# Starting five output groups of the second branch's projection among its last attention head

## The chip, the cores and the metric

The kernel runs on one core of a Trainium2 chip. The core has five engines: TensorE (PE, matrix products and their weight loads, PEld), VectorE (DVE), ScalarE (ACT), GpSimd (POOL) and SyncE (SP, which issues the transfers here). The metric is the time of one execution on the device in microseconds (us); lower is better.

## The reference

Two layers of a transformer-like trunk over 512 latent tokens and 256 context tokens of width 1024. Each layer has two parallel attention branches that share one input projection; each branch is gated and projected, and the two are merged and projected once more:

```python
def _merge(a_att, b_att, a_z, b_z, g_a, g_b, w_o_a, w_o_b, w_out):
    o_a = (a_att * jax.nn.silu(a_z)) @ w_o_a
    o_b = (b_att * jax.nn.silu(b_z)) @ w_o_b
    merged = jax.nn.sigmoid(g_a) * o_a + jax.nn.sigmoid(g_b) * o_b
    return merged @ w_out
```

Branch A is neighbourhood attention with 8 heads of width 64. Branch B is grouped-query attention with 8 query heads and 2 key/value heads; its latent queries read all 768 tokens. In the first layer the context tokens go through the same computation and read only context; in the second only the latent tokens are updated. The output is the 512 latent tokens.

## The kernel before

All matrices are kept as a high and a low part (`hi`, `lo`), and a product is three matmuls: hi x hi, hi x lo, lo x hi (`mm3`, lines 341 to 343). A 512-column matmul fills one bank of PSUM, the accumulator memory, which has eight. Activations stand with channels on the 128 partitions, so that the 512 channels of a branch are four row tiles k = 0 to 3, and `hilo` makes the two parts of a row tile: a copy on ACT (line 543, `gbh` for branch B) and a subtraction on POOL (line 544, `gbl`). `load_w2` loads weights and splits them in the same way; the lo part alternates between POOL and DVE (line 328).

**The last stage of a layer.** The 8 query heads of branch B go through `pipeline`. Head h's scores (lines 704 and 705, into score tiles `pss` of two banks each, two buffers) are computed while head h - 1's values are: for each of six key tiles, four transposes on PE into a `pst` bank (line 655), a hi copy on ACT (`pth`, 658), a lo subtraction on DVE (`ptl`, 659), and two value matmuls that add to the one `psv` bank (958 and 959). At the end of a head `head_out` copies half of `psv` on ACT (667), adds on DVE (668), which frees the bank, and multiplies into `zb` on POOL (669). Two heads make one row tile of `zb`, so that its fourth tile is whole only after head 7, the last. In the first layer each head also has context queries, with a score tile, two values matmuls of 256 columns for each half (732 and 733), and a `head_out` of their own. Between heads PE does pieces of a list of other projections, `fill`, each piece in the one `psf` bank. After the fill has run out, `early` makes hi and lo parts of row tiles 0 to 2.

**The second output projection** (`w_o_b`) comes next, in a new set of banks: `open_ps(x=5)` closes the score and values pools and gives five banks `psx` besides `psf`. Its output has eight row tiles f; with the column spans (0 to 512, and 512 to 768 in the first layer) that is 16 output groups in the first layer and 8 in the second. A group is `chan_proj`: k = 0 to 3, three matmuls each, then `evac_b` on DVE and ACT, which takes the bank with `tg` (lines 993 and 994) and makes the hi and lo parts of the merged activations (`mh`, `ml`). Then follows the final projection (`w_out`, `tok_proj`, also `psf` and `psx` banks).

The order in the program is not the order in which Python calls are made: a scheduler puts the instructions of each engine in an order by its own timeline, and each engine then runs its list strictly in that order, waiting where a source is not ready or a buffer not free. With it, the group in the `psf` bank stood among the last heads' values before the change already.

Of the kernel before, what the change touches and what calls it, by code (L numbers as in the profile page):

```python
# [11 lines left out]
ALU = mybir.AluOpType  # L12
# [27 lines left out]
def R(ap):  # L40
    return ap.bitcast(F32R)
# [7 lines left out]
def hybrid_kernel(es: ExitStack, tc, x, ctx, cvec, w_ada, w_ada0, small, gvec, w_in, w_o_a, w_o_b, w_out,  # L49
                  bias_int, bias_edge, rope, ident_d, out):  # L50
    nc = tc.nc
    V, S, G, T = nc.vector, nc.scalar, nc.gpsimd, nc.tensor
# [265 lines left out]
    def load_w2(src, col0, nk, lo_eng):  # L318

        res = []  # L320
        for i in range(nk // 2):
            raw = raw_tile()
            nc.sync.dma_start(raw.rearrange("p (k n) -> p k n", k=2),
                              src[256 * i:256 * i + 256, col0:col0 + 256].rearrange("(k p) n -> p k n", k=2))
            hi = wp.tile([128, 512], F32R, tag="whi", name=nm("whi"), bufs=8)
            S.copy(hi, raw)  # L326
            lo = wp.tile([128, 512], F32R, tag="wlo", name=nm("wlo"), bufs=8)
            lo_eng(i).tensor_tensor(lo, raw, F(hi), ALU.subtract)  # L328
            res += [(hi[:, c:c + 256], lo[:, c:c + 256]) for c in (0, 256)]
        return res  # L330
# [3 lines left out]
    mix_lo = lambda k: V if k % 2 == 1 else G  # L334
# [23 lines left out]
    def chan_proj(w, f, a, n0, n1, evac):  # L358

        ps = psw(n1 - n0)  # L360
        nk = len(w)
        for k in range(nk):
            hi, lo = a(0, k), a(1, k)
            mm3(ps, (w[k][0][:, 128 * f:128 * f + 128], w[k][1][:, 128 * f:128 * f + 128]),
                (R(hi[:, n0:n1]), R(lo[:, n0:n1])), k == 0, k == nk - 1)
        evac(f, n0, n1, ps)

    def start_mods(q):
        cuts = (0, 256, 512, 768) if q == 0 else (0, 768)
# [23 lines left out]
    def run(fill, n):  # L393
        for _ in range(min(n, len(fill))):
            fill.pop(0)()
# [80 lines left out]
    def layer(l, hx, nxt, mid):  # L476
# [4 lines left out]
        spans = [(0, 512), (512, 768)] if first else [(0, 512)]  # L481
# [53 lines left out]
        gated = {}  # L535

        def hilo_tiles(name):
            return [big(name + part).rearrange("p (f n) -> p f n", f=4) for part in "hl"]

        def hilo(src, dst, fs):  # L540
            sv = src.rearrange("p (f n) -> p f n", f=4)
            for f in fs:
                S.copy(R(dst[0][:, f, :ntok]), sv[:, f, :ntok])
                G.tensor_tensor(R(dst[1][:, f, :ntok]), sv[:, f, :ntok], dst[0][:, f, :ntok], ALU.subtract)
# [4 lines left out]
        def o_chunks(br, prepare, evac):  # L549

            src = (w_o_a if br == "a" else w_o_b)[l]
            act = lambda part, k: gated[br][part][:, k, :]
            res = []
            for i in range(4):
                st = {}

                def ld(i=i, st=st):
                    st["w"] = load_w2(src, 256 * i, 4, mix_lo)
                pieces = [lambda f=f, n0=n0, n1=n1, i=i, st=st:
                          chan_proj(st["w"], f, act, n0, n1, lambda f, a, b, ps: evac(2 * i + f, a, b, ps))  # L560
                          for f in range(2) for n0, n1 in spans]
                res.append((ld, ([prepare] if i == 0 and prepare else []) + pieces))
            return res
# [9 lines left out]
        def tg_part(c, f, n0, n1):  # L573
            return tg[2 * (f // 4) + c].rearrange("p (f n) -> p f n", f=4)[:, f % 4, n0:n1]
# [7 lines left out]
        if first:  # L582
            w, pss = [], [psw() for t in range(6)]
# [19 lines left out]
        else:  # L603
            hp["p"] = bgp_es.enter_context(tc.tile_pool(name=f"cp{l}", bufs=1, reuse_waits="tile"))
            w = load_w(W, C_AK, 512, KT, mix_lo)
# [30 lines left out]
        if True:  # L636
# [183 lines left out]
                head_out(po, e, zv[64 * e:64 * e + 64, h // 2, 0:512])  # L820
                return vsl

            def pipeline(fill, spread, scores_of, values_of, last=None, bg=[]):

                n = len(fill)
                prev = None
                for h in range(8):
                    att["bg"] = bg if h > 3 or pm["n"] == 1 else []
                    st = scores_of(h)
                    if prev is not None:  # L830
                        values_of(h - 1, prev)
                    run(fill, len(fill) - (n - n * min(h + 1, spread) // spread))
                    prev = st
                if last is not None:
                    run(fill, len(fill))
                    last()
                run(bg, len(bg))
                values_of(7, prev)
                run(fill, len(fill))

            akt = [k_tile(e, True) for e in range(2)]

# [8 lines left out]
            def values_of(dst, f):  # L851
                def g(h, st):
                    vsl = f(h, st[0])
                    if first:
                        e = h % 2
                        zv = dst.rearrange("p (f n) -> p f n", f=4)
                        ctx_values(st[1], vsl, zv[64 * e:64 * e + 64, h // 2, 512:768], e)
                return g
# [116 lines left out]
                gated["b"] = hilo_tiles("gb")  # L975
                hilo(zb, gated["b"], range(3))
            bg = gate_steps((1,), att["p"]) if first else []
            pipeline(fill, 8, gq_first, values_of(zb, gq_values), early, bg)
            gq_es.close()

        with tc.tile_pool(name=f"mrg{l}", bufs=1, reuse_waits="tile") as mp:
            open_ps(x=5)
            extra = lambda name: mp.tile([128, 3072], F32, tag="extra", name=nm(name))
            gv = mp.tile([128, nv, DM], F32, tag="gate", name=nm("gate"), bufs=1)
            for v in range(nv):
                src = gd[l][8 * v:8 * v + 8].rearrange("k p -> (k p)").unsqueeze(0)
                nc.sync.dma_start(gv[:, v, :], src.to_broadcast([128, DM]))
            hilo(zb, gated["b"], [3])
            mg = []

            def evac_b(f, n0, n1, ps):
                a, b = tg_part(0, f, n0, n1), tg_part(1, f, n0, n1)
                V.scalar_tensor_tensor(b, b, 1.0, ps, ALU.add, ALU.mult)
                V.tensor_tensor(a, a, b, ALU.add)
                hi, lo = [m[:, f % 4, n0:n1] for m in mg[f // 4]]
                S.copy(R(hi), a)
                V.tensor_tensor(R(lo), a, hi, ALU.subtract)
            chunks = o_chunks("b", None, evac_b)
            chunks[0][0]()
            for i in range(4):  # L1000
                if i < 3:
                    chunks[i + 1][0]()
                if i % 2 == 0:
                    mg.append(hilo_tiles("m"))
                for piece in chunks[i][1]:
                    piece()

            nt = 6 if first else 4
            xv = [a.rearrange("p (t n) -> p t n", t=3) for a in (big("xt0"), extra("xt1"))]
            xts = []  # L1010
            for t in range(nt):
                xt = xv[t // 3][:, t % 3, :]
                nc.sync.dma_start(xt, x_src(t) if first else xs1[128 * t:128 * t + 128, :])
                xts.append(xt)
            a_m = lambda part, k: mg[k // 4][part][:, k % 4, :]
            bg = ada_steps(1, range(16), (1,), 2, mp) + [lambda: ada_mod(1)] if first else []
            run(bg, 1)
            per_bg = -(-len(bg) // nt)
# [123 lines left out]
```

## Time and profile before

| | |
|---|---|
| timed runs | 1154.26, 1154.82 and 1156.4 us; median 1154.82 |
| profiled execution, first to last instruction (span) | 1153.4 us; its own time is not listed apart, the median of the runs is 1.4 us longer than the span |
| mean granted TensorE clock | 0.998 of full speed |
| PE busy | 1123.0 us, 97% of the span |
| DVE, ACT, POOL busy | 809.8, 573.9, 495.0 us |

The last head of branch B ends at about 567 us of the span in the first layer and at about 1085 us in the second. In the lines of the profile, a timeline row gives start and duration in us, engine, line, operation, output <- inputs, shape, and in brackets how long the engine idled before it and what ended that. Matmuls are pipelined: their rows overlap, and the step from one start to the next is what a matmul costs PE. PE counts as busy while one of its matmuls is in flight. A row of windows gives the stretch, its length, then busy time and count of PE, PEld, DVE, ACT and POOL, the granted clock, the share of the DMA engines and GB/s.

### The profile page before, as it was taken

The numbers are of one execution on the slowest core, as the hardware profiler recorded it, in microseconds if no ns is written. First come the engines' busy times: TensorE is split into PE (matmuls) and PEld (weight loads), VectorE is DVE, ScalarE is ACT, GpSimd is POOL, SyncE is SP. The second block draws the span as 40 slices with busy tenths as digits, with TensorE's granted clock in tenths as the row PEclk, the third lists the DMA queues.
The fourth block names the chain that finished last, engine by engine and source line by source line (L and its number), as shares of the span: only waits on it lengthen the run. The fifth ranks groups of instructions, "written<-read, shape, count | busy, mean of one in ns | idle before, by whom it ended". The sixth has DMA issues, their size and how long they took to land.

```text
span 1153.4 us, 17280 instructions
## 1 busy us (share of the span) xinstructions
PE 1123.0 (97%) x6078; PEld 949.0 (82%) x6078; DVE 809.8 (70%) x1508; ACT 573.9 (50%) x1167; POOL 495.0 (43%) x459
## 2 busy tenths in 40 slices
PE   5999999999999999999999999999999999999998
PEld 4688888889988888878788787888888988887786
DVE  4566688897464687688587755469787665898563
ACT  5453266666433465566330265346666445766521
POOL 3362354454375243354411126245553664465311
PEclk9999999999999999999999999999999999999999
DMA  9644222233342332470353523543332333142143
GB/s 368 195 126 137 69 85 65 72 115 97 115 130 63 107 102 73 67 276 19 121 172 101 174 74 110 176 106 113 108 105 84 110 101 101 65 173 92 63 129 92
DMA packets 88000, 134.04 MB, mean 116 GB/s; under 512 B 10629, under 2 KB 52585, under 8 KB 86249
## 3 DMA queue, kind: packets, MB, share of 16 engines
q1 hardware_dynamic: 87912, 132.94, 36.8%
q8 instruction: 48, 0.79, 0.3%
q14 instruction: 40, 0.32, 0.1%
HBM read 115.58 MB, written 17.32 MB: 115 GB/s over the span
## 4 chain that ended last, share of the span: by engine, by line
PE 83%; DVE 7%; issue 3%; POOL 2%; ACT 2%; DMA 2%; ACTq 0%; POOLq 0%; DVEq 0%
PE psx L341 12%; PE psx L343 12%; PE psx L342 12%; PE psf L341 9%; PE psf L342 9%; PE psf L343 9%; PE pst L655 5%; PE pss L704 2%; PE pss L705 2%; PE psv L959 2%; PE psv L958 1%; PE pss L781 1%; PE pst L417 1%; DVE wlo L328 1%; DVE ptl L659 1%
## 5 line engine op out<-in xcount | busy, mean ns | idle before, releaser
L659 DVE TENSOR_TENSOR ptl<-pst,pth 128x512 fp32r<-128x512 f32 (+1 forms) x176 | 116.0, 672 | 46.4 <-ACT pth L658 45.4
L658 ACT CAST pth<-pst 128x512 fp32r<-128x512 f32 (+1 forms) x176 | 99.2, 576 | 87.5 <-PE pst L655 56.3
L328 POOL TENSOR_TENSOR wlo<-raw,whi 128x512 fp32r<-128x512 f32 x68 | 95.0, 1402 | 108.9 <-ACT whi L326 87.8
L341 PE MATMUL psf<-hx,whi 128*128 128x512 f32 (+1 forms) x368 | 139.2, 378 | 0.0
L342 PE MATMUL psf<-hx,whi 128*128 128x512 f32 (+1 forms) x368 | 138.1, 375 | 0.0
L343 PE MATMUL psf<-hx,wlo 128*128 128x512 f32 (+1 forms) x368 | 137.8, 374 | 0.0
L341 PE MATMUL psx<-whi,hx 128*128 128x512 f32 (+1 forms) x368 | 137.2, 374 | 0.0
L342 PE MATMUL psx<-wlo,hx 128*128 128x512 f32 (+1 forms) x368 | 135.8, 369 | 0.0
L343 PE MATMUL psx<-whi,hx 128*128 128x512 f32 (+1 forms) x368 | 133.6, 369 | 0.0
L314 POOL TENSOR_TENSOR wlo<-raw,whi 128x512 fp32r<-128x512 f32 x44 | 60.4, 1373 | 140.4 <-ACT whi L311 123.8
L311 ACT CAST whi<-raw 128x512 fp32r<-128x512 f32 x96 | 58.7, 623 | 103.5 <-PE psx L343 38.6
L326 ACT CAST whi<-raw 128x512 fp32r<-128x512 f32 x136 | 82.5, 622 | 50.3 <-DMA raw<-in_w_in_dram 34.1
L655 PE MATMUL pst<-ident,p 128*128 128x128 f32 x640 | 99.9, 272 | 1.4 <-DVE ptl L659 0.9
L328 DVE TENSOR_TENSOR wlo<-raw,whi 128x512 fp32r<-128x512 f32 x68 | 70.2, 1033 | 28.3 <-ACT whi L326 27.8
L655 PEld LDWEIGHTS pst<-ident,p 128*128 128x128 f32 x640 | 77.7, 141 | 13.3 <-DVE ptl L659 1.6
L644 POOL TENSOR_SCALAR r<-r 128x1 f32<-128x1 f32 x64 | 23.1, 361 | 151.7 <-DVE r L639 144.1
L645 POOL TENSOR_TENSOR p<-p,r 128x512 f32<-128x512 f32 (+1 forms) x64 | 83.5, 1304 | 5.0
L341 PEld LDWEIGHTS psx<-whi,hx 128*128 128x128 f32 x368 | 69.6, 189 | 11.8 <-issue 0.8
L343 PEld LDWEIGHTS psf<-hx,wlo 128*128 128x128 f32 x368 | 69.4, 188 | 11.8
L343 PEld LDWEIGHTS psx<-whi,hx 128*128 128x128 f32 x368 | 69.4, 189 | 11.5
L342 PEld LDWEIGHTS psx<-wlo,hx 128*128 128x128 f32 x368 | 69.6, 189 | 11.0
L341 PEld LDWEIGHTS psf<-hx,whi 128*128 128x128 f32 x368 | 69.4, 189 | 10.8 <-ACT zt L502 0.2
(239 smaller groups left out, 3033.4 us busy)
## 6 DMA issues: line engine op xcount, KB each, us to landing
raw<-in_w_in_dram SPq DMA_DIRECT2D x168, 256.0 KB, 2.9
rawb<-in_w_ada_dram SPq DMA_DIRECT2D x64, 256.0 KB, 2.8
gs<-zt SPq DMA_DIRECT2D x32, 256.0 KB, 2.0
raw<-in_w_out_dram SPq DMA_DIRECT2D x32, 256.0 KB, 2.8
tg<-gs SPq DMA_DIRECT2D x4, 1536.0 KB, 7.4
rawx<-in_w_ada_dram SPq DMA_DIRECT2D x4, 1024.0 KB, 7.2
rawy<-in_w_ada_dram SPq DMA_DIRECT2D x4, 1024.0 KB, 12.2
raw<-in_w_o_a_dram SPq DMA_DIRECT2D x16, 256.0 KB, 2.7
```

The lines of the kernel that those rows point to most:

```text
L311: S.copy(hi[:, :n], raw[:, :n])
L314: e.tensor_tensor(lo[:, :n], raw[:, :n], F(hi[:, :n]), ALU.subtract)
L326: S.copy(hi, raw)
L328: lo_eng(i).tensor_tensor(lo, raw, F(hi), ALU.subtract)
L341: T.matmul(ps, lhs[0], rhs[0], start=first, stop=False)
L342: T.matmul(ps, lhs[0], rhs[1], start=False, stop=False)
L343: T.matmul(ps, lhs[1], rhs[0], start=False, stop=last)
L644: G.tensor_scalar(r[:, i:i + 1], r[:, i:i + 1], 0.5, None, ALU.mult)
L645: G.tensor_tensor(p[:, c0:c1], p[:, c0:c1], r[:, i:i + 1].to_broadcast([128, c1 - c0]), ALU.mult)
L655: T.transpose(pt[:, c0:c0 + 128], src, ident)
L658: S.copy(hi[:, n0:n1], pt[:, n0:n1])
L659: V.tensor_tensor(lo[:, n0:n1], pt[:, n0:n1], F(hi[:, n0:n1]), ALU.subtract)
```

## The change

`chan_proj` is split, so that a group can be begun with some row tiles and ended later (`chan_mm`). `pipeline` gets a `tail`, called after the last head's values. There, still with the pools of the attention stage, `begin_b` opens five groups: one in the `psf` bank, and one each in halves of score tiles. It issues row tiles 0 to 2 of each. Then come the hi and lo parts of row tile 3, and for each of the five its last row tile and its evacuation. The other groups follow as before in the new set of banks, with weights loaded one chunk ahead.

```diff
+    def chan_mm(ps, w, f, a, n0, n1, k0, k1):
+        for k in range(k0, k1):
             hi, lo = a(0, k), a(1, k)
             mm3(ps, ...)
...
                 values_of(7, prev)
                 run(fill, len(fill))
+                if tail is not None:
+                    tail()
...
+            ob = []
+            def begin_b():
+                w, act = [], lambda part, k: gated["b"][part][:, k, :]
+                room = [(psw(1024, "s"), c) for _ in range(2) for c in (0, 512)]
+                for f in range(8):
+                    for n0, n1 in spans:
+                        if len(ob) == 5:
+                            return
+                        if f // 2 == len(w):
+                            w.append(load_w2(w_o_b[l], 256 * len(w), 4, mix_lo))
+                        if ob:
+                            bank, c = room[len(ob) - 1]
+                            ps = bank[:, c:c + n1 - n0]
+                        else:
+                            ps = psw(n1 - n0)
+                        chan_mm(ps, w[f // 2], f % 2, act, n0, n1, 0, 3)
+                        ob.append((f, n0, n1, ps, w[f // 2]))
+            pipeline(fill, 8, gq_first, values_of(zb, gq_values), early, bg, begin_b)
...
+            hilo(zb, gated["b"], [3])
+            for f, n0, n1, ps, w in ob:
+                chan_mm(ps, w, f % 2, act_b, n0, n1, 3, 4)
+                evac_b(f, n0, n1, ps)
             gq_es.close()
...
-            hilo(zb, gated["b"], [3])
...
-            chunks = o_chunks("b", None, evac_b)
...
+            for f in range(8):
+                for n0, n1 in spans:
+                    if (f, n0) in [o[:2] for o in ob]:
+                        continue
+                    for i in range(f // 2, min(f // 2 + 2, 4)):
+                        if i not in wb:
+                            wb[i] = load_w2(w_o_b[l], 256 * i, 4, mix_lo)
+                    chan_proj(wb[f // 2], f % 2, act_b, n0, n1, ...)
```

What this does to PE's list is shown at three places. In the rows of the changed kernel the value matmuls carry lines 962 and 963 (958 and 959 before) and the transposes 657 (655); the matmuls of `mm3` keep 341 to 343.

**PE, second layer, end of the last head.** Before: psv_11708 is that head's values bank, psf_11818, psx_11835, psx_11864 and psx_11881 are output groups, whi and wlo their weights; whi_11794 holds row tiles 0 and 1, whi_11800 row tiles 2 and 3.

```order
L958 MATMUL psv_11708<-pth_11769,vb_9656 128x512
L959 MATMUL psv_11708<-ptl_11770,vb_9656 128x512
L341 MATMUL psx_11835<-gbh_11700,whi_11794 128x512
L342 MATMUL psx_11835<-gbl_11701,whi_11794 128x512
L343 MATMUL psx_11835<-gbh_11700,wlo_11796 128x512
```

Three groups' row tiles 0 to 2 follow here, 24 matmuls, and only then the first that reads row tile 3, into psf_11818. Now, with psf_11795, pss_11779 and pss_11780 as the early groups (whi_11791 and whi_11822 hold their row tiles 2 and 3):

```order
L962 MATMUL psv_11708<-pth_11769,vb_9656 128x512
L963 MATMUL psv_11708<-ptl_11770,vb_9656 128x512
L341 MATMUL psf_11795<-gbh_11700,whi_11791 128x512
L341 MATMUL pss_11779<-gbh_11700,whi_11791 128x512
L341 MATMUL pss_11780<-gbh_11700,whi_11822 128x512
L342 MATMUL psf_11795<-gbl_11701,whi_11791 128x512
L343 MATMUL psf_11795<-gbh_11700,wlo_11793 128x512
```

The last value matmul is now followed at once by matmuls that read row tile 3. The groups in the third and fourth score tile (pss_11781 and pss_11782) stand 21 rows further on, complete, behind a new group in the psf bank.

**PE, second layer, the last values of head 5** (psv_11419; psv_11583 is head 6, whose first transposes go to pst_11584). Before:

```order
L959 MATMUL psv_11419<-ptl_11470,vb_9656 128x512
L655 MATMUL pst_11584<-ident,p_11374 128x128
L655 MATMUL pst_11584<-ident,p_11386 128x128
L655 MATMUL pst_11584<-ident,p_11399 128x128
L655 MATMUL pst_11584<-ident,p_11411 128x128
L958 MATMUL psv_11419<-pth_11480,vb_9656 128x512
L959 MATMUL psv_11419<-ptl_11481,vb_9656 128x512
```

Now:

```order
L657 MATMUL pst_11584<-ident,p_11411 128x128
L341 MATMUL pss_11780<-gbh_11700,whi_11816 128x512
L342 MATMUL pss_11780<-gbl_11701,whi_11816 128x512
L343 MATMUL pss_11780<-gbh_11700,wlo_11818 128x512
L341 MATMUL pss_11780<-gbh_11700,whi_11816 128x512
L342 MATMUL pss_11780<-gbl_11701,whi_11816 128x512
L343 MATMUL pss_11780<-gbh_11700,wlo_11818 128x512
L962 MATMUL psv_11419<-pth_11480,vb_9656 128x512
L963 MATMUL psv_11419<-ptl_11481,vb_9656 128x512
```

Six matmuls of the group in the second score tile have come between head 6's first transposes and head 5's last two value matmuls. The other twelve that moved stand at four other places among the values of heads 5 and 6; none stands among those of head 7.

**PE, first layer, behind the last head's context values** (psv_6344). Before:

```order
L732 MATMUL psv_6344<-pth_6340,vb_3447 128x256
L733 MATMUL psv_6344<-ptl_6341,vb_3447 128x256
L341 MATMUL psx_6410<-gbh_6256,whi_6369 128x256
L342 MATMUL psx_6410<-gbl_6257,whi_6369 128x256
L343 MATMUL psx_6410<-gbh_6256,wlo_6371 128x256
```

Now:

```order
L734 MATMUL psv_6344<-pth_6340,vb_3447 128x256
L735 MATMUL psv_6344<-ptl_6341,vb_3447 128x256
L341 MATMUL psf_6369<-gbh_6256,whi_6365 128x512
L341 MATMUL pss_6353<-gbh_6256,whi_6365 128x256
L341 MATMUL pss_6354<-gbh_6256,whi_6365 128x512
L342 MATMUL psf_6369<-gbl_6257,whi_6365 128x512
```

Here, too, row tiles 0 to 2 of two groups (pss_6353, 256 columns, and pss_6354, 512) have moved ahead of the context values, and the matmuls of row tile 3 follow at once.

More of the change, by code (lines that the diff above doesn't have):

```diff
@@ L360, in chan_proj @@
         ps = psw(n1 - n0)
-        nk = len(w)
-        for k in range(nk):
+        chan_mm(ps, w, f, a, n0, n1, 0, len(w))
+        evac(f, n0, n1, ps)
+    def chan_mm(ps, w, f, a, n0, n1, k0, k1):
+        for k in range(k0, k1):
             hi, lo = a(0, k), a(1, k)
             mm3(ps, (w[k][0][:, 128 * f:128 * f + 128], w[k][1][:, 128 * f:128 * f + 128]),
-                (R(hi[:, n0:n1]), R(lo[:, n0:n1])), k == 0, k == nk - 1)
-        evac(f, n0, n1, ps)
+                (R(hi[:, n0:n1]), R(lo[:, n0:n1])), k == 0, k == len(w) - 1)
     def start_mods(q):
@@ L821, in na_values, with pipeline @@
                 return vsl
-            def pipeline(fill, spread, scores_of, values_of, last=None, bg=[]):
+            def pipeline(fill, spread, scores_of, values_of, last=None, bg=[], tail=None):
                 n = len(fill)
@@ L977, in layer, with evac_b @@
             bg = gate_steps((1,), att["p"]) if first else []
-            pipeline(fill, 8, gq_first, values_of(zb, gq_values), early, bg)
+            ob = []
[16 more added lines that the diff above has]
+            pipeline(fill, 8, gq_first, values_of(zb, gq_values), early, bg, begin_b)
+            mg = []
+            def evac_b(f, n0, n1, ps):
+                if f // 4 == len(mg):
+                    mg.append(hilo_tiles("m"))
+                a, b = tg_part(0, f, n0, n1), tg_part(1, f, n0, n1)
+                V.scalar_tensor_tensor(b, b, 1.0, ps, ALU.add, ALU.mult)
+                V.tensor_tensor(a, a, b, ALU.add)
+                hi, lo = [m[:, f % 4, n0:n1] for m in mg[f // 4]]
+                S.copy(R(hi), a)
+                V.tensor_tensor(R(lo), a, hi, ALU.subtract)
+            act_b = lambda part, k: gated["b"][part][:, k, :]
+            hilo(zb, gated["b"], [3])
+            for f, n0, n1, ps, w in ob:
+                chan_mm(ps, w, f % 2, act_b, n0, n1, 3, 4)
+                evac_b(f, n0, n1, ps)
             gq_es.close()
@@ L987, in layer @@
                 nc.sync.dma_start(gv[:, v, :], src.to_broadcast([128, DM]))
-            hilo(zb, gated["b"], [3])
[L989 to L997, printed above, removed]
-            chunks = o_chunks("b", None, evac_b)
[L999 to L1006, printed above, removed]
+            wb = {o[0] // 2: o[4] for o in ob}
+            for f in range(8):
[5 more added lines that the diff above has]
+                            wb[i] = load_w2(w_o_b[l], 256 * i, 4, mix_lo)
+                    chan_proj(wb[f // 2], f % 2, act_b, n0, n1, lambda _, a, b, ps: evac_b(f, a, b, ps))
             nt = 6 if first else 4
```

## The prediction

> **What bounds the kernel now.** I read the page first, then the windows over the two places the change touches (the end of the second branch's last head in each layer), then the timeline there. Page, busy time by engine and the chain that ended last:
>
> ```profile
> PE 1123.0 (97%) x6078; PEld 949.0 (82%) x6078; DVE 809.8 (70%) x1508; ACT 573.9 (50%) x1167; POOL 495.0 (43%) x459
> PE 83%; DVE 7%; issue 3%; POOL 2%; ACT 2%; DMA 2%; ACTq 0%; POOLq 0%; DVEq 0%
> ```
>
> TensorE (PE) is busy 97% of the span and carries 83% of the chain. So an edit that keeps the number of matmuls, as this one does, is worth only the PE idle time that it removes or makes. Where there is some, by stretch (PE busy, weight loads, DVE, ACT, POOL):
>
> ```profile
> 565.00:570.00 5.00, 3.01 (x18) 2.27 (x18) 1.82 (x3) 1.07 (x3) 3.99 (x4) 1.00 0.32 98
> ...
> 1080.00:1085.00 5.00, 4.71 (x23) 3.03 (x22) 2.77 (x4) 1.92 (x4) 0.18 (x1) 1.00 0.23 66
> 1085.00:1090.00 5.00, 5.00 (x23) 4.12 (x23) 0.69 (x1) 1.55 (x3) 3.05 (x3) 1.00 0.11 42
> ```
>
> In layer 0 PE is busy 3.01 us of 565 to 570. In layer 1 it falls to 23 matmuls and 3.03 us of weight loads from 1080 to 1085, within the last head's values, and is back at the full rate (4.12 us of loads) right after. The timeline shows what it does there; first the end of the last head in layer 1 (start, duration, engine, line, output and inputs):
>
> ```profile
> 1084.24 0.50 PE L959 MATMUL psv<-ptl,vb 128*128 128x512 f32 x1 [0.22 <-DVE ptl L659]
> ...
> 1084.58 0.40 PE L341 MATMUL psx<-gbh,whi 128*128 128x512 f32 x1
> ...
> 1087.54 0.62 ACT L543 CAST gbh<-zb 128x512 fp32r<-128x512 f32 x1 [2.12 <-POOL zb L669]
> ...
> 1088.23 1.29 POOL L544 TENSOR_TENSOR gbl<-zb,gbh 128x512 fp32r<-128x512 f32 x1 [0.73 <-ACT gbh L543]
> ...
> 1090.06 0.39 PE L341 MATMUL psf<-gbh,whi 128*128 128x512 f32 x1
> ```
>
> The last value matmul starts at 1084.24. Behind it runs a chain through ACT, DVE, POOL, ACT and POOL again that makes the fourth row tile of the second branch's activations: the head output, then its hi part (gbh, ready at 1088.16), then its lo part (gbl, ready at 1089.52), 5.3 us in all. PE is never idle meanwhile: it has the first three row tiles of three output groups, 24 matmuls from 1084.58 to 1090.06 (0.228 us each), ahead of the first one that needs the fourth tile, and at 1090.06 that tile has been there for 0.5 us. **Before the change the chain is wholly covered, by the kind of matmul that the change takes away from there.**
>
> **The change part by part.** The new order of PE shows three early groups, not five: the list of rooms asks for a new score tile in each of its four passes and the score pool has two buffers, so the third and fourth wait until the first two are evacuated. One of the three (in the psf bank) was early before too. So 18 matmuls of 512 columns move from behind the last head to ahead of it in layer 1; in layer 0 nine of 512 and nine of 256.
>
> *Layer 1, behind the last value.* Only three hi matmuls of the fourth tile now stand ahead of the first that needs its lo part, and they need the hi part. With the chain at its old length PE stands from 1084.58 to about 1088.2, works 0.7 us and stands again until 1089.6: 5.0 less 3 x 0.228, so 4.3 us of new idle time. The chain's operations keep their engines and order. One weight split that POOL now does ahead of an earlier head's product falls where POOL waits for DVE, so I cost it at nothing (1.3 us, the length of POOL's rows here, if that cover went).
>
> *Layer 1, ahead of it.* The 18 need 18 x 0.228 = 4.1 us of PE. What falls into time in which PE waited anyway is a gain. PE's waits among the rows where they are put:
>
> ```profile
> 1063.19 0.41 PE L958 MATMUL psv<-pth,vb 128*128 128x512 f32 x1
> 1065.14 0.50 PE L959 MATMUL psv<-ptl,vb 128*128 128x512 f32 x1 [1.54 <-DVE ptl L659]
> ...
> 1069.11 0.47 PE L959 MATMUL psv<-ptl,vb 128*128 128x512 f32 x1
> ...
> 1071.16 0.50 PE L958 MATMUL psv<-pth,vb 128*128 128x512 f32 x1
> ...
> 1072.58 0.48 PE L958 MATMUL psv<-pth,vb 128*128 128x512 f32 x1
> 1073.07 0.50 PE L959 MATMUL psv<-ptl,vb 128*128 128x512 f32 x1
> ...
> 1074.07 0.40 PE L958 MATMUL psv<-pth,vb 128*128 128x512 f32 x1
> 1074.48 0.51 PE L959 MATMUL psv<-ptl,vb 128*128 128x512 f32 x1
> ```
>
> The big wait, 1.7 us before 1065.14, is for DVE, and one moved matmul stands ahead of it: 0.23 us swallowed. Eleven more come before the last value matmul of head 5 (1069.11). From there to the first of head 6 (1071.16) a chain runs over ACT and DVE that frees the one values bank, 2.05 us, with PE idle for about 1 us of it; the eleven stand ahead of its start, so they push it and fill nothing of it (I allow 0.16, since ACT was still at an earlier copy). Two stand ahead of the wait at 1074.48, and they and the shift remove that wait and the one at 1073.07. By the steps between rows (0.49 and 0.41 where 0.32 and 0.23 are normal, and 0.11 each for the restart) that is 0.28 + 0.29. The last four push the end of head 6 again. Swallowed: 0.23 + 0.16 + 0.28 + 0.29 = 0.96 us. None of the 18 stands inside the last head, where PE's waits stay. So the last value matmul comes 4.1 - 0.96 = 3.1 us later. In sum 4.1 us come off behind the head, 3.1 are added ahead of it and 4.3 of idle time are new: **+3.3 us** (+0.2 if all 18 were swallowed, +4.3 if none).
>
> *Layer 0.* Here POOL paces the chain:
>
> ```profile
> 560.29 5.87 POOL L544 TENSOR_TENSOR gbl<-zb,gbh 128x768 fp32r<-128x768 f32 x3 [3.60 <-PE psf L342]
> ...
> 566.22 0.50 PE L342 MATMUL psf<-gbl,whi 128*128 128x512 f32 x1 [0.79 <-POOL gbl L544]
> ...
> 567.27 0.28 PE L341 MATMUL psx<-gbh,whi 128*128 128x256 f32 x1
> 567.39 0.28 PE L342 MATMUL psx<-gbl,whi 128*128 128x256 f32 x1
> ...
> 568.82 0.36 ACT L667 COPY ho<-psv 64x256 f32<-64x256 f32 x1 [3.10 <-POOL zb L669]
> ...
> 571.40 1.85 POOL L544 TENSOR_TENSOR gbl<-zb,gbh 128x768 fp32r<-128x768 f32 x1 [0.95 <-ACT gbh L543]
> ...
> 573.66 0.40 PE L342 MATMUL psf<-gbl,whi 128*128 128x512 f32 x1
> ...
> 600.12 0.40 PE L341 MATMUL psx<-whi,mh 128*128 128x512 f32 x1
> ```
>
> POOL makes three lo parts from 560.29 (it had waited for a matmul of the first projection) and more behind them, the last one done at 573.25. PE takes that up at 573.66 and works without a stop to 600.12, the start of the final projection: 26.46 us. Moving matmuls forward does not start POOL earlier; two of them (one of 256, one of 512 columns, 0.35 us) even stand ahead of the matmul that POOL waits for. The 18 take 9 x 0.228 + 9 x 0.12 = 3.1 us, of which about 1.3 falls into PE's waits for the earlier lo parts (0.79 us idle before 566.22, and smaller ones). So the context values end at about 569.1 instead of 567.27, too late for ACT's copy at 568.82, which then goes 0.6 us later. The last lo part follows at 573.85, so the matmul of 573.66 comes 0.2 us later. Behind it there are 162 matmuls instead of 152, the ten more of 256 columns at 0.12 us: 1.2 us. New PE waits of about 2.9 and 1.3 us, ahead of the hi and the lo part, replace the old ones. **+1.4 us** (+0.8 if the chain kept its time, +2.7 if none of the 3.1 us were swallowed).
>
> The final projection of layer 0 and the start of layer 1 keep their order, names of banks aside. PE's waits for weights there (in total, times, longest):
>
> ```profile
> PE psx L341 <- ACT whi L311: 0.3, 1, 0.3
> PE psx L342 <- POOL wlo L314: 0.3, 1, 0.3
> ```
>
> With the restart these cost PE up to 0.9 us, which could be swallowed if those loads did not shift along. But they go into buffers that PE itself frees, so I take nothing off and keep 0.9 for the range. Early banks must now be evacuated before the third and fourth score tile and the next psf group start; 12 matmuls lie between and an evacuation is one DVE operation, so 0 (up to 0.3 a layer). The one load of output weights that moves up has nobody waiting for it.
>
> **Sum.** 1.4 + 3.3 = 4.7 us. The profiled span is 1153.4 us and the median of the timed runs 1154.82; the 1.4 us between them the change doesn't touch. So 1158.1 us in the span and **1159.5 us** timed.
>
> **Rivals.**
> *Not slower (7%).* ACT and DVE, not PE, pace the last three heads of layer 1, and the moved matmuls vanish in PE's waits. Place: the stretch from 1063.19 to 1084.24, with 1.7 us of waiting before 1065.14, about 1 us at each change of head, and some 1.3 us in the last one (5 x (1 - 3.03 / 4.12) by its weight loads): about 5, more than the 4.1 moved. It decides if that stretch (21.05 us) grows by less than 1 us. Then layer 1 costs 0.2 and layer 0 0.8, less the 0.9 at the weights: 0.1, 1155.0 us. Against it: the waits are not where the matmuls are put, and 15 of the 18 stand ahead of a chain of fixed length.
>
> *The clock drops (20%).* One long wait of PE in this trace is followed by half speed:
>
> ```profile
> 19.11 1.94 PE L287 MATMUL pst<-ident,x 128*128 128x128 f32 x8 [2.92 <-DVE x L283]
> ...
> 20.00:21.00 1.00, 1.00 (x6) 0.50 1.00 418
> 24.00:25.00 1.00, 1.00 (x9) 1.00 0.97 412
> ```
>
> After 2.92 us of idle time the granted clock is 0.50 at 20 to 21, and 1.00 again at 24. The new waits are 3.6 us in layer 1 and 2.9 in layer 0, while the 1.7 us before 1065.14 cost no clock. If the low state lasts some 3.4 us (between the 1 and 5 us that these rows allow), PE loses half of that, 1.7 us: 1161.2, and 1162.9 if both waits do it. One drop shows that it can happen and not how often, so it gets less than half. The Trainium skill (TensorE: Matmul & The Clock Gate, "Why this matters for your kernels") has a rule against such a change: no gaps of more than about 3 us between bursts of matmuls, since a window of idleness halves the clock. By that rule the time would be this rival's; the trace agrees with it in the drop above.
>
> *Something gains (4%).* At most PE's idle time at the two places could go, 2.0 us of 565 to 570 (5 less 3.01) and 1.3 in the last head: 1151.5. For it stands nothing that I found; against it, that behind 1090 PE works at the full rate, so no wait is left there to remove.
>
> **How the numbers follow.** The forecast has 69%. With every bound to one side its own range would be 1157.1 (twice 0.96 swallowed, layer 0 at 0.8, 0.9 off at the weights) to 1162.4. The range goes from 1157.2 to 1162.0 and leaves out the not slower and the faster case and the far end of the clock's. A measurement of this kernel can tell some 0.2% from no change, 2.3 us, so slower means above 1157.1: nearly all of the forecast and the clock's 20%, 0.88. Same is the first rival and the forecast's edge, 0.08; faster 0.04.
>
> **What would show it.** Right: in layer 1 PE idle some 3.6 us and then 0.7 between the last value matmul and the first lo matmul of the fourth tile, released by ACT gbh and POOL gbl; the stretch that was 21.05 us 3 us longer; in layer 0 PE idle some 3 us behind the context values. Wrong: no such wait, score tiles three and four among the values, or the last value at its old distance. A clock under 1.00 behind either wait is the second rival.

## The result and the profile after

The changed kernel takes 1165.11 us (median of 4 runs, 1163.46 to 1167.04) against 1155.28 us before in the same set: a ratio of 1.0084, 95% interval 1.0069 to 1.0098. It is slower, as forecast, but by 9.8 us instead of 4.7, and outside the range. The profiled execution spans 1163.1 us (1153.4 before), with a mean granted clock of 0.992 (0.998 before). From the page, busy time by engine and the chain that ended last:

```profile
PE 1128.3 (97%) x6078; PEld 953.9 (82%) x6078; DVE 810.3 (70%) x1508; ACT 574.7 (49%) x1167; POOL 494.5 (43%) x459
PE 80%; DVE 8%; issue 3%; DMA 2%; POOL 2%; ACT 2%; SPq 0%; ACTq 0%; POOLq 0%; DVEq 0%
```

The number of matmuls is the same, yet PE is busy 5.3 us longer: the same matmuls take longer somewhere. The timeline says where. The end of the last head in the second layer, of the changed kernel (start, duration, engine, line, output and inputs, idle time before and what ended it):

```profile
1091.68 0.49 PE L963 MATMUL psv<-ptl,vb 128*128 128x512 f32 x1 [0.23 <-DVE ptl L661]
1092.26 0.58 ACT L669 COPY ho<-psv 64x512 f32<-64x512 f32 x1 [1.36 <-PE psv L963]
...
1094.94 0.62 ACT L545 CAST gbh<-zb 128x512 fp32r<-128x512 f32 x1 [2.10 <-POOL zb L671]
1095.61 0.79 PE L341 MATMUL psf<-gbh,whi 128*128 128x512 f32 x1 [3.44 <-ACT gbh L545]
1095.63 1.27 POOL L546 TENSOR_TENSOR gbl<-zb,gbh 128x512 fp32r<-128x512 f32 x1 [0.73 <-ACT gbh L545]
...
1096.95 0.28 PEld L342 LDWEIGHTS psf<-gbl,whi 128*128 128x128 f32 x1 [0.42 <-POOL gbl L546]
1097.05 0.69 PE L342 MATMUL psf<-gbl,whi 128*128 128x512 f32 x1
1097.55 0.63 PE L343 MATMUL psf<-gbh,wlo 128*128 128x512 f32 x1
1097.97 0.63 PE L342 MATMUL pss<-gbl,whi 128*128 128x512 f32 x1
```

The chain of the fourth row tile is as long as before (last value matmul to the end of gbl: 5.2 us, 5.3 before), and PE now stands for 3.44 us of it. What follows is the second thing to see: from 1097.55 to 1097.97 is a step of 0.42 us where 0.23 is normal. In layer 0, with the start of the final projection as the last row:

```profile
569.33 0.28 PE L735 MATMUL psv<-ptl,vb 128*128 128x256 f32 x1
572.24 0.80 PE L341 MATMUL psf<-gbh,whi 128*128 128x512 f32 x1 [2.63 <-ACT gbh L545]
...
574.13 0.80 PE L342 MATMUL psf<-gbl,whi 128*128 128x512 f32 x1 [0.46 <-POOL gbl L546]
574.73 0.63 PE L343 MATMUL psf<-gbh,wlo 128*128 128x512 f32 x1
575.15 0.41 PE L342 MATMUL pss<-gbl,whi 128*128 128x256 f32 x1
...
604.05 0.40 PE L341 MATMUL psx<-whi,mh 128*128 128x512 f32 x1
```

The same again: 2.63 us of waiting, then steps of 0.42 us. The windows of the changed kernel, cut where its granted clock changes (PE busy, weight loads, DVE, ACT, POOL, PEclk, DMA share, GB/s):

```profile
568.74:572.16 3.42, 0.87 (x6) 0.61 (x4) 0.43 (x1) 1.17 (x2) 1.51 (x2) 1.00 0.82 237
572.16:575.57 3.41, 2.87 (x7) 2.08 (x8) 0.18 (x1) 0.03 (x1) 1.81 (x1) 0.50 0.88 287
575.57:578.98 3.41, 3.41 (x15) 3.17 (x15) 3.41 (x7) 0.93 (x2) 0.00 (x0) 0.50 1.02 408
...
1090.98:1094.40 3.42, 0.96 (x3) 0.34 (x2) 1.34 (x2) 0.58 (x1) 0.76 (x1) 1.00 0.44 153
1094.40:1097.81 3.41, 2.20 (x5) 1.59 (x6) 0.00 (x0) 0.62 (x1) 1.77 (x2) 0.50 0.00 0
1097.81:1101.22 3.41, 3.41 (x9) 2.64 (x9) 2.97 (x5) 1.24 (x2) 0.00 (x0) 0.50 0.00 0
```

Each wait leaves a window in which PE is busy for 0.9 to 1.0 us of 3.4, and two windows at a clock of 0.50 follow, 6.8 us each time. The kernel before has no such window between 25 and 1150 us.

### The profile page after: what moved, and what is told of

Its sections match the earlier page's. It is cut to its first block, busy times and chain, and to the rows that moved or that the text cites. A ratio compares the mean times of both kernels' runs of the same rounds, so it can differ in the third digit from the quotient of the medians.

```text
span 1163.1 us, 17282 instructions
## 1 busy us (share of the span) xinstructions
PE 1128.3 (97%) x6078; PEld 953.9 (82%) x6078; DVE 810.3 (70%) x1508; ACT 574.7 (49%) x1167; POOL 494.5 (43%) x459
## 4 chain that ended last, share of the span: by engine, by line
PE 80%; DVE 8%; issue 3%; DMA 2%; POOL 2%; ACT 2%; SPq 0%; ACTq 0%; POOLq 0%; DVEq 0%
PE psx L342 11%; PE psx L343 11%; PE psx L341 11%; PE psf L341 9%; PE psf L342 9%; PE psf L343 9%; PE pst L657 4%; PE pss L706 2%; PE pss L707 2%; PE psv L963 2%; PE pss L783 1%; PE psv L962 1%; PE pst L419 1%; DVE wlo L328 1%; DVE ptl L661 1%
## 5 line engine op out<-in xcount | busy, mean ns | idle before, releaser
L341 PEld LDWEIGHTS psx<-whi,hx 128*128 128x128 f32 x368 | 69.7, 190 | 11.9 <-issue 0.8
L342 PEld LDWEIGHTS psx<-wlo,hx 128*128 128x128 f32 x368 | 69.7, 189 | 11.1
```

The source lines that it names most:

```text
L341: T.matmul(ps, lhs[0], rhs[0], start=first, stop=False)
L342: T.matmul(ps, lhs[0], rhs[1], start=False, stop=False)
```

## The experiments

All times are medians in us; each kernel is compared with the kernel before in its own set (1155.3 to 1155.9). The theory is that of the prediction's second rival, the **clock theory**: the forecast's 4.7 us plus half-clock time behind both waits. Its rival is that waits and moved matmuls alone cost 9.8 and the clock is a by-product. Beside it stands the **cover theory**: early matmuls do no harm by themselves, what costs is that nothing is left for the wait.

**Fill the waits, first try.** PE gets work whose result nobody reads, into an unused half of a score tile:

```diff
+                att["lo"] = lo
...
                         ob.append((f, n0, n1, ps, w[f // 2]))
+                        if len(ob) == 3:
+                            for _ in range(9 if first else 13):
+                                T.matmul(room[0][0][:, 512:1024], R(vb[:, 5, 1, 0:128]), att["lo"], start=True, stop=True)
```

> The changed kernel with 9 (layer 0) and 13 (layer 1) extra matmuls of 512 columns that multiply the last head's last lo part into an unused half of a score tile, behind the last value matmul: 2.1 and 3.0 us of work with no use, inside waits of 2.6 and 3.4 us. They change no wait and no order on the other engines' way to the fourth row tile. Clock theory: the changed kernel's 9.8 us are the 4.7 us forecast (new idle time, moved matmuls not swallowed, ten more narrow matmuls behind the last lo part in layer 0) and about 5 us in which PE works at half clock, 2.4 us behind layer 0's wait and 2.5 behind layer 1's. With the waits filled the clock stays at 1.00, so about 1160.2 us against 1165.1, mean clock back at 0.998. Rival, the waits and the moved matmuls alone cost 9.8 and the low clock is a by-product: 1165.1 or a little more.

Measured: 1165.04, ratio 1.0079 (1.0066 to 1.0092), clock 0.996. A miss: the number is the one that the rival gave. But the trace shows why: in layer 0 the scheduler put the 9 fillers ahead of the context values (last one at 571.75 instead of 569.33), so the chain there began later and the clock still fell. In layer 1 they stood where they should and no low clock followed: from the last value matmul to the end of the span 69.6 us, against 71.4 in the changed kernel.

**One layer at a time.** `begin_b` is passed on in one layer only:

```diff
-            pipeline(fill, 8, gq_first, values_of(zb, gq_values), early, bg, begin_b)
+            pipeline(fill, 8, gq_first, values_of(zb, gq_values), early, bg, begin_b if first else None)
```

> The change in layer 0 alone; layer 1 has the order of the kernel before. The trace of the changed kernel puts the start of the final projection of layer 0 3.9 us later than before. Clock theory: 1155.3 + 4.0 = 1159.3, one half-clock stretch behind the wait. Forecast without a clock: 1155.3 + 1.4 = 1156.7.

> The change in layer 1 alone. From the trace of the changed kernel, layer 1 takes 3.4 us ahead of the last value matmul and 2.3 behind it. Clock theory: 1155.3 + 5.7 = 1161.0. Forecast without a clock: 1155.3 + 3.3 = 1158.6. If the two layers' costs don't add (one sets the other's state), the two single-layer kernels will not sum to 9.8.

Measured: 1160.05, ratio 1.0037 (1.0024 to 1.0050), for layer 0 alone, and 1160.13, ratio 1.0039 (1.0027 to 1.0051), for layer 1 alone. That is 4.7 and 4.8 us, 9.4 in sum against 9.8 with both, so the layers' costs add. Both have one half-clock stretch of 6.8 us, each behind its own wait. Both lie nearer to the clock theory than to the forecast, layer 1 1 us under the expectation.

**Cover put back.** Groups four and five get the free halves of the two score tiles, and a small matmul that needs the last head's last lo part holds them behind it:

```diff
+                att["lo"] = lo
...
-                room = [(psw(1024, "s"), c) for _ in range(2) for c in (0, 512)]
+                room = [(b, c) for b in [psw(1024, "s") for _ in range(2)] for c in (0, 512)]
+                room = [room[i] for i in (0, 2, 1, 3)]
...
+                        if len(ob) > 2:
+                            T.matmul(ps[:, 0:128], R(vb[:, 5, 1, 0:128]), att["lo"][:, 0:128], start=True, stop=True)
                         chan_mm(ps, w[f // 2], f % 2, act, n0, n1, 0, 3)
```

> As the changed kernel, three groups early, but groups four and five get the two unused halves of the two score tiles, and their first three row tiles are held back behind the last value matmul by one small matmul each of 128 columns that needs the last head's last lo part: 18 useful matmuls stand in the wait. Cover theory (the early matmuls are harmless, what costs is that nothing is left for the wait): layer 1 ahead of the last value +3.2, behind it 4.1 less work and 0.3 of waits and small matmuls, so -0.6; layer 0 likewise some -0.6; no low clock: about 1154.1 against 1155.3 of the kernel before. Rival, the early matmuls themselves do the harm, by pushing the heads' values: not under 1160.

Measured: 1159.66, ratio 1.0037 (1.0024 to 1.0050). A miss by 5.5 us, and by the number alone the rival's. In layer 0 the held groups again stood ahead of the context values and pushed the chain, and one window at half clock followed there. In layer 1 the heads took 3.5 us longer and the tail gave back 1.4, not 3.8. So it was run in layer 1 alone, with layer 0 as before:

> The covered order, three groups early and 18 matmuls of two more held back behind the last value, in layer 1 alone, with the kernel before's order in layer 0. From the profile of the covered order in both layers: +3.5 ahead of the last value, -1.3 behind it, 1.00 clock: 1157.8, against 1160.1 for the change in layer 1 alone and 1155.6 before. If the cover is worth nothing: 1160.

Measured: 1157.59, ratio 1.0019 (1.0011 to 1.0028), clock 0.998. Its timeline and its waits of PE behind the last head:

```profile
1088.22 0.50 PE L964 MATMUL psv<-ptl,vb 128*128 128x512 f32 x1 [0.23 <-DVE ptl L661]
...
1092.93 0.39 PE L341 MATMUL psf<-gbh,whi 128*128 128x512 f32 x1
1093.61 0.46 PE L342 MATMUL psf<-gbl,whi 128*128 128x512 f32 x1
```

```profile
PE psf L341 <- DVE tg L1013: 1.4, 1, 1.4
```

With the same 18 matmuls early, the wait for the fourth tile is gone and so is the low clock: 2.5 us off the change in layer 1 alone. It still does not reach the kernel before: the early matmuls lengthen the heads by 3.4 us, and the tail gives back only 1.4 (1156.0 - 1088.22 = 67.8 us against 1153.4 - 1084.24 = 69.2). One reason is new: five banks now become ready together, and PE waits 1.4 us for DVE's evacuations; the rest was not split.

**No early group, but no cover either.** The kernel before (`begin_b` is not passed on), with each of these groups' row tiles in the order 3, 0, 1, 2:

```diff
-        for k in range(k0, k1):
+        ks = [3, 0, 1, 2] if pm.get("late") else list(range(k0, k1))
+        for k in ks:
...
-            pipeline(fill, 8, gq_first, values_of(zb, gq_values), early, bg, begin_b)
+            pipeline(fill, 8, gq_first, values_of(zb, gq_values), early, bg, None)
...
+                    pm["late"] = True
                     chan_proj(wb[f // 2], f % 2, act_b, n0, n1, lambda _, a, b, ps: evac_b(f, a, b, ps))
+                    pm["late"] = False
```

> The order of the kernel before, no group begun early, but each output group of the second projection starts with the fourth row tile instead of ending with it, so that nothing can stand in the wait. Cover theory: the wait costs without any early matmul: layer 1 +4.1 and +1.8 by the clock, layer 0 +5.5 and +2.3, about 1169 (1166 to 1170). Rival, the harm comes from the matmuls put among the heads' values: at most 1157.

Measured: 1169.45, ratio 1.0116 (1.0101 to 1.0132). Its rows at the end of layer 1's last head:

```profile
1093.47 0.50 PE L964 MATMUL psv<-ptl,vb 128*128 128x512 f32 x1 [0.22 <-DVE ptl L662]
1097.42 0.50 PE L341 MATMUL psf<-gbh,whi 128*128 128x512 f32 x1 [3.44 <-ACT gbh L546]
```

The same wait of 3.44 us without a single early matmul, and a worse time. So the harm is in the lost cover, and the changed kernel, with its matmuls done early, loses less (1.0084 against 1.0116).

**Fewer and more early groups.** Two instead of three (the psf bank and one score tile), and five, with the list of rooms mended:

```diff
-                room = [(psw(1024, "s"), c) for _ in range(2) for c in (0, 512)]
+                room = [(psw(1024, "s"), 0)]
...
-                        if len(ob) == 5:
+                        if len(ob) == 2:
```

```diff
-                room = [(psw(1024, "s"), c) for _ in range(2) for c in (0, 512)]
+                room = [(b, c) for b in [psw(1024, "s") for _ in range(2)] for c in (0, 512)]
```

> Two early groups instead of three: the one that was early before too, and one in a score tile, so 9 matmuls a layer are moved instead of 18. The order shows that the one open score tile already keeps all other groups behind the fourth row tile. Cover theory: the price is that of the wait, not of the number moved: 1164.5 to 1166. Rival, each moved matmul has its price: halfway, 1160.

> The change with its list of rooms mended: two score tiles in four halves, so that five groups are early as its words say, 36 matmuls a layer moved instead of 18. Cover theory: the waits stay as they are, uncovered, the further 18 come off behind and are added ahead, less up to 1 us that falls into waits: 1164 to 1165.5. Rival, what is missing is only the other two groups: near or under the 1155.3 of the kernel before.

Measured: two 1170.66, ratio 1.0128 (1.0114 to 1.0142); five 1164.05, ratio 1.0073 (1.0060 to 1.0085). Five is as expected: doing what the words of the change say repairs nothing. Two is 5 us worse than I expected. I had held the price of the wait for a constant; but each group that is not early then comes behind the wait, and 9 matmuls a layer are 2 us. In the traces, from the cast of the table below to the final projection and from the value row there to the end, two early groups cost 6.1 us in layer 0 and 7.0 in layer 1 (and 1.1 between them, where their order had changed), three 3.5 and 5.7, and none of them early, in the kernel without cover, 6.9 and 7.2. So with two the wait is as uncovered as with none, and the two times (ratios 1.0128 and 1.0116, overlapping intervals) can't be told apart; with three and five less is left behind the wait.

**One early group.** That of the psf bank, as before the change: the loop stops at one group and asks for no score tile, so none is held open:

> The changed program with one early group, that of the psf bank, which was early before as well; no group in a score tile. The order shows 24 matmuls of three other groups behind the last value matmul of layer 1, as in the kernel before. Cover theory: nothing is lost, 1155.6 within 1.5. Rival, the rearranged code itself (a third tile of the activations split earlier, other places for the loads) costs: 1158 or more.

Measured: 1157.33, ratio 1.0019 (1.0010 to 1.0028), between the two expectations. At the place of the change it costs nothing (from the last value matmul of layer 1, at 1086.93, to the end of its span of 1156.0 it is 69.1 us, 69.2 before). The 1.9 us arose elsewhere: in the trace the rows ahead of the first branch of layer 1, at 760 us, stand 0.5 us later than before and those behind it, at 890, 2.5 us later, and the order of the rows on POOL, DVE and ACT between them had changed. What in them costs it, I did not test.

**Fill the waits, second and third try.** In layer 0 four small matmuls read the last context head's output, so they can't stand ahead of its values. In layer 1 first 6, then 13 fillers:

```diff
+                att["lo"] = lo
...
+                att["ho"] = t1[m:m + 64, :n], ident[m:m + 64]
...
+                        if len(ob) == 3 and first:
+                            for _ in range(4):
+                                T.matmul(room[0][0][:, 512:768], att["ho"][1], att["ho"][0], start=True, stop=True)
+                        if len(ob) == 3 and not first:
+                            for _ in range(6):    # 13 in the third try
+                                T.matmul(room[0][0][:, 512:1024], R(vb[:, 5, 1, 0:128]), att["lo"], start=True, stop=True)
```

> The changed kernel with less work of no use, and in layer 0 behind the context values instead of ahead of them: there 4 matmuls of 256 columns on the last context head's output, in layer 1 only 6 of 512 columns (1.4 us of the 3.4 us wait), so about 2 us of that wait stay. Clock theory, with a threshold: the clock is halved behind a window of 3.4 us in which PE is busy for less than about half; with these fillers the window ahead of layer 1's drop goes from 0.28 to about 0.68 busy. No low clock, no other time changed: 1165.1 - 4.0 = 1161.1. Rival, any wait of 2 us brings the low clock: 1163 or more, with half-clock rows behind 1095. If only layer 0's filler is too short: 1163.3.

Measured: 1163.34, ratio 1.0068 (1.0056 to 1.0081). Layer 0 kept its clock. In layer 1 the guess of 0.68 was wrong, and usefully so; the time is the rival's, 1163 or more:

```profile
1090.49 1.55 PE L1008 MATMUL pss<-ptl,vb 128*128 128x512 f32 x6
1094.10 0.50 PE L341 MATMUL psf<-gbh,whi 128*128 128x512 f32 x1 [2.05 <-ACT gbh L545]
...
1095.46 0.50 PE L342 MATMUL psf<-gbl,whi 128*128 128x512 f32 x1 [0.41 <-POOL gbl L546]
```

```profile
1088.99:1092.40 3.41, 2.82 (x10) 1.61 (x9) 1.39 (x2) 0.97 (x2) 0.27 (x1) 1.00 0.46 154
1092.40:1095.82 3.42, 1.31 (x5) 0.81 (x6) 0.00 (x0) 0.62 (x1) 2.28 (x2) 1.00 0.00 0
1095.82:1099.23 3.41, 3.41 (x10) 2.67 (x9) 2.77 (x5) 1.24 (x2) 0.00 (x0) 0.50 0.00 0
```

In this run the grid of the clock lies so that the fillers fall into one window and what is left of the waits, 2.05 and 0.41 us, into the next, which is busy for 0.38 and is followed by one window at half clock. So a wait of 2 us was enough here.

> The changed kernel with both waits filled by work of no use where it delays nothing: 4 small matmuls behind layer 0's context values (the filling that kept the clock at 1.00 there), 13 of 512 columns behind layer 1's last value (the filling that kept it there). Clock theory: only the waits and the matmuls that weren't swallowed are left, layer 0 +1.7, layer 1 +3.6 ahead of the last value and +0.5 behind it: 1161.5, no half-clock row between 50 and 1150 us. Rival, the low clock costs nothing: 1165.

Measured: 1162.34, ratio 1.0060 (1.0047 to 1.0072), no half-clock row between 50 and 1150 us. Its rows at both places, with the first value row of the three heads that take the early matmuls (the four small matmuls stand as eight rows):

```profile
570.87 1.99 PE L1005 MATMUL pss<-ho,ident 64*128 64x256 f32 x8 [0.97 <-DVE ho L671]
...
574.43 0.50 PE L342 MATMUL psf<-gbl,whi 128*128 128x512 f32 x1 [0.80 <-POOL gbl L546]
...
602.53 0.40 PE L341 MATMUL psx<-whi,mh 128*128 128x512 f32 x1
...
1057.71 0.40 PE L964 MATMUL psv<-pth,vb 128*128 128x512 f32 x1
...
1090.90 0.50 PE L965 MATMUL psv<-ptl,vb 128*128 128x512 f32 x1 [0.23 <-DVE ptl L661]
1091.24 3.15 PE L1008 MATMUL pss<-ptl,vb 128*128 128x512 f32 x13
1094.88 0.50 PE L341 MATMUL psf<-gbh,whi 128*128 128x512 f32 x1 [0.50 <-ACT gbh L545]
```

From the first lo matmul to the final projection of layer 0 it takes 602.53 - 574.43 = 28.10 us, 29.92 in the changed kernel: 1.8 us by the clock. From the last value matmul of layer 1 to the end 69.7 us, against 71.4: 1.7 by the clock. Between the medians (by ratio 1.0084 and 1.0060) it is 2.8 us. So the low clock costs some 3 us, not the 5 that the clock theory gave it, and the rest, some 6 to 7, is waits and matmuls: **the clock is a third of the loss and not all that the forecast missed.** Of the five timed runs one, 1163.88 us, has a mean clock of 0.995 where the others have 0.997 to 0.999, so the filling may not have kept the clock in every run, and 2.8 may be too little.

## Why the prediction was right or wrong

Two more rows of each kernel, ahead of the change in layer 0 and ahead of the three heads that take the early matmuls in layer 1, make an account (before, then after):

```profile
543.33 0.84 ACT L543 CAST gbh<-zb 128x768 fp32r<-128x768 f32 x1 [0.65 <-POOL zb L669]
1054.51 0.40 PE L958 MATMUL psv<-pth,vb 128*128 128x512 f32 x1
```

```profile
543.73 0.84 ACT L545 CAST gbh<-zb 128x768 fp32r<-128x768 f32 x1 [0.65 <-POOL zb L671]
1058.52 0.40 PE L962 MATMUL psv<-pth,vb 128*128 128x512 f32 x1
```

Differences to the kernel before, in us, each from two starts (the same cast in the filled kernel is at 544.00):

| stretch | forecast | after | both waits filled |
|---|---|---|---|
| up to the cast, ahead of the change | 0 | 0.40 | 0.67 |
| cast to the last lo part taken up, layer 0 | 0.2 | 0.07 | 0.10 |
| from there to the final projection | 1.2 | 3.46 | 1.64 |
| final projection to the value row above | 0 | 0.08 | 0.79 |
| that row to the last value matmul, layer 1 | 3.1 | 3.43 | 3.46 |
| last value matmul to the end | 0.2 | 2.26 | 0.54 |
| sum | 4.7 | 9.70 | 7.20 |

The first and the fourth line come without an order that would explain them, and I read them as what one execution differs from another: the traces of the experiments that keep the order there lie between 0.65 less and 0.77 more in the first (3.4 more in the kernel without cover, whose clock rose a window later at the start), and between 0.82 less and 0.79 more in the fourth.

**What bounds it, and the cover: right.** PE stands 3.44 us, released by ACT gbh, and then 0.42 by its weight load, released by POOL gbl (forecast 3.6 and 0.7), and 2.63 and 0.46 in layer 0 (2.9 and 1.3). The kernel without early groups and without cover shows that the lost cover is the harm.

**The early matmuls in layer 1: right in kind, 0.3 us short.** 4.1 us were moved, 3.43 arrived, so 0.67 was swallowed, not 0.96. The term that failed is the pair of small waits in head 6:

```profile
1077.50 0.51 PE L962 MATMUL psv<-pth,vb 128*128 128x512 f32 x1 [0.58 <-DVE ho L670]
...
1078.91 0.48 PE L962 MATMUL psv<-pth,vb 128*128 128x512 f32 x1
1079.40 0.50 PE L963 MATMUL psv<-ptl,vb 128*128 128x512 f32 x1
...
1084.31 0.40 PE L963 MATMUL psv<-ptl,vb 128*128 128x512 f32 x1
```

The step of 0.49 at 1079.40 is still there (it was that of 1073.07), since the matmuls stand behind it. Head 6 is 6.81 us long instead of 5.70: 1.11 for six matmuls of 1.37, so 0.26 was swallowed and not 0.57.

**Layer 0 behind the last lo part: 0.4 us short without the clock,** 1.64 instead of 1.2. Ten matmuls of 256 columns are 1.2; most of the rest is the term that the forecast put at 0 with up to 0.3 a layer allowed, the evacuation of the early banks. In the kernel with both waits filled:

```profile
575.47 0.40 PE L343 MATMUL pss<-gbh,wlo 128*128 128x512 f32 x1
575.93 0.19 PEld L341 LDWEIGHTS psf<-gbh,whi 128*128 128x128 f32 x1 [0.51 <-DVE tg L1017]
575.94 0.39 PE L341 MATMUL psf<-gbh,whi 128*128 128x256 f32 x1
576.16 0.28 PE L342 MATMUL psf<-gbl,whi 128*128 128x256 f32 x1
```

The next psf group waits until DVE has taken the bank: steps of 0.47 and 0.22 where 0.23 and 0.12 are normal, 0.34 us. **The tail of layer 1: 0.3 short,** 0.54 instead of 0.2; the same place costs 0.14 there (steps of 0.26 and 0.34 from 1097.50), the rest was not split. So the forecast's own 4.7 us were 5.7 (0.10 + 1.64 + 3.46 + 0.54).

**The clock: the step that failed.** The forecast took the clock at 1.00 behind both waits. That put at nothing what measured 3.5 us in the traces (1.82 and 1.72) and 2.8 between the medians, the largest part of the 5.6 us that it missed by. It gave the rival 20%, since "One drop shows that it can happen and not how often". But the wait that had halved the clock in the trace was 2.92 us, and the new ones were put at 3.6 and 2.9: the only row near them spoke for a drop, and the 1.7 us wait that cost none was the farther one. The rival should have been the forecast. Its price, 1.7 us each, was nearly met, 1.8 and 1.7, but by accident: the low state lasted 6.8 us each time instead of 3.4, and until the lo part came, at 1097.05 and 574.13, PE would have stood anyway. The Trainium skill (TensorE: Matmul & The Clock Gate, "Why this matters for your kernels") asks for no gaps of more than about 3 us. That rule would have called layer 1 rightly, and the trace is stricter: a gap of 2.63 us halved the clock in layer 0, and one of 2.05 with 0.41 behind it in the kernel with 6 fillers.

With the rival's time, 1162.9, the forecast would still have been 2.2 us low: 1.0 us are the terms above, 0.1 the clock, 0.5 the two lines of the table that no order explains, and 0.6 the distance from the profiled span to the median, 2.0 us here and 1.4 before.

## What to carry to other kernels

Before work is moved ahead of a chain, ask what PE does while the chain runs: matmuls that look like a late start may be the cover of a wait, and a score tile held open for one early group can keep every other group from being that cover. A new wait on PE is to be priced with the clock behind it, by the rows nearest in length; filling the wait with work of no use tells the two prices apart in one run, if that work can't be put ahead of what the wait is for.

## What the runs showed of the clock

I had not expected how cleanly the windows tell it. In every trace the clock changes only at points a multiple of 3.41 us apart. Cut on that grid, in the thirteen traces of this case and between 50 and 1140 us, all 13 windows at full clock in which PE was busy for 0.11 to 0.48 of the time were followed by half clock, and none of some 4100 others, all of which have 0.54 or more. Three of the nearest, from the kernel without cover, from the one with a single early group and from the kernel before:

```profile
565.76:569.18 3.42, 1.65 (x8) 0.96 (x7) 2.14 (x4) 1.54 (x3) 3.42 (x2) 1.00 0.22 77
569.18:572.59 3.41, 1.22 (x4) 0.93 (x4) 0.82 (x3) 0.36 (x1) 2.82 (x3) 0.50 0.21 73
```

```profile
1064.51:1067.92 3.41, 1.86 (x11) 1.30 (x9) 3.41 (x5) 1.82 (x4) 3.41 (x3) 1.00 0.21 77
1067.92:1071.33 3.41, 3.41 (x20) 2.85 (x21) 1.61 (x4) 1.96 (x4) 2.07 (x4) 1.00 0.46 135
```

```profile
1063.35:1066.77 3.42, 1.88 (x14) 1.43 (x12) 2.33 (x3) 0.82 (x2) 3.42 (x3) 1.00 0.54 155
```

To come back takes more: at half clock, windows busy for 0.36 to 0.84, and one with 0.86, were followed by another one at half clock; one with 0.85 and all from 0.89 on by full speed. In these traces every single wait of PE of 1.9 us or more was followed by half clock, or lay in it, and none of fifteen from 1.3 to 1.6 us was. But a wait of 1.30 us with a second behind it in the same window was followed by it too (cover put back in both layers, layer 0, busy for 0.46). So it is the sum in one window that tells, and where the grid lies decides what falls into one; a wait of 2 us that the grid splits, without loss of clock, no run here shows. A second small wait behind the first can prolong the low state. (The ends of matmuls are modelled, so these shares are not exact to the last digit.)
